# Kernel study: the 24 gate outputs of the first layer as one fp32 product in four column groups

## The chip, the cores and the metric

The kernel runs on one core of one Trainium2 chip. The metric is the device time of one execution in microseconds (us), lower is better; the median of 3 runs stands for the kernel. A separate, profiled execution gives the trace.

## The reference, cut to what matters

One inference step of a two-layer decoder trunk for 544 tokens (512 of a prompt, 8 x 4 of samples), width 1024, all in fp32. Layer 0 mixes with mLSTM heads and GLA heads, layer 1 with a Mamba-2 mixer; an MLP and layer norms follow each. Only the input projection of layer 0 matters here:

```python
mq, mk, mv, mo, mi, mf, gq, gk, gv, gg, ga = split((x @ w_in), AB_SPLITS)   # w_in: 1024 x 3096
ig = mi + ig_bias                                   # 4 columns: input gates
lf = log_sigmoid(mf + fg_bias)                      # 4 columns: forget gates
la = log_sigmoid(ga @ wa2 + ba) / GLA_TAU           # ga: 16 columns, the GLA decay
```

Of the 3096 outputs, 3072 make 24 tiles of 128 rows; the other 24 (`mi`, `mf`, `ga`) are the gates.

## The kernel before, in words

Everything is kept transposed: 128 features on the partitions, tokens along the free dimension. The 544 tokens are worked in two halves of 272 (`hf` 0 and 1). A dense product of fp32 accuracy is made of three products of a rounded type: weights and input are cut into a high and a low part (`whi`, `wlo`, `xh`, `xl`), and hi·hi, hi·lo and lo·hi are added up in PSUM. One weight tile (128 outputs, 1024 inputs, so eight blocks of K) therefore costs 24 products per half and 48 in all (`dense`, L357). The high part is made by ScalarE (a cast, L166 for weights, L286 for x), the low part by VectorE (a subtraction, L167 and L287).

`WeightStream` (L116) loads the weight tiles in a planned order through SyncE's queue into three raw buffers (`wraw`) and five pairs of cut buffers. `take_x` (L290) loads the first half of x in four pieces through ScalarE's queue, and cuts the first weight tile and these pieces by turns, a quarter of the weight tile and a quarter of x at a time. Loads on the hardware queues carry one of eight completion counters, given out by turns: a load that takes a counter up again waits until the load that had it before has landed.

The stage `ab` (L706) is the input projection with the mixer heads beside it. Its tiles go, by `order` (L821), gate, gq 0-1, gk 0-1, gv 0-3, mq, mk, mv, gg, mo. The first five tiles (`HEAD`) are worked half by half: all five for hf 0, then all five for hf 1; the others tile by tile. The gate tile is a whole weight tile of which 24 columns are used, at 0-3 (mi), 32-35 (mf) and 64-79 (ga); ScalarE evacuates it with a bias into `gate` (L797).

TensorE's instructions are in the order in which the program writes them. The mixer work is written as "lanes": generators that `tick` (L338) moves on, one step per dense product, each lane waiting as many products as its `yield` says. `warm` (L1367) is a lane too: it puts products of ones (L1372, fp32, 128x128, two records each) ahead of the first dense products and between their groups of six, so that TensorE isn't idle while data arrive. The GLA lane (L1336) waits until the gate tile is ready for both halves, waits 12 products more, and issues the decay products `la` (L1001, gate times wa2, K = 128) for q = 0 and, 12 products on, q = 1 (`gla_decay`); then it waits for the tiles gq 1 and gk 1 and goes into `gla_scores`: products `gd` (L1037), and then, every 15 dense products, one level of products `gs` (L1065).

Between `la` and the first `gs` lies a chain over three engines: ScalarE takes Abs, Exp and Ln of `la` (tile `lat`, L1002 to L1005), VectorE the minimum, a subtraction and a scan along the tokens (tile `A`, L1003 to L1007), GpSimd the difference tile `F` (L1048), ScalarE two Exp of it (L1050, L1051), and VectorE two multiplications (`zq`, L1055, and `zk`, L1057), which the first `gs` reads. ScalarE, VectorE and GpSimd have fixed orders of their own, found by the scheduler when the program is built; what they do there beside the chain are weight cuts, evacuations, masks of q (`qm`, L1032) and copies of the gate rows (`rw`, `uw`, L1184, L1185).

Of the kernel before, what the change touches and what calls it, by code (L numbers as in the profile page):

```python
# [34 lines left out]
W = dict(dec=12, gates=30, gr=8, sc=16, lev=14, v=24, kd=10, out=38, ss=40, end=12, c0=20, u=13, s=16, ml=12, mr=40, dt=238, sg=72, sx=14, sq=26, so=48, l0=12, l1=12, v0=74, v1=55, f0=16, f1=18, f2=4, ls=20, vs=47)  # L35
LEVELS = (64, 32, 16, 8, 4, 2, 1)
# [191 lines left out]
def trunk_kernel(ctx, tc, a, stages=("ab", "mlp0", "ssd", "mlp1")):  # L228
# [22 lines left out]
    for st in stages:  # L251
        if st == "ab":
            for w in [a["ab_gate"]] + [a["ab_in"][b] for b in range(24)]:
                ws.plan("ab", w)
# [35 lines left out]
    def take_x(pool, bufs=12):  # L290
# [8 lines left out]
        with tc.high_priority(), tc.manual_schedule(engines=order):  # L299
            ts = [load(S, 0, k)[0] for k in range(0, KT, 2)]  # L300
            S.preload_act_table_set("natural_log_exp_and_others")
            ws._emit([lambda k=k: cut(0, 2 * k, ts[k]) for k in range(KT // 2)])
            ws.ahead(HEAD)
            for k in range(0, KT, 2):
                t, loaded = load(nc.sync, 1, k)
                cut(1, k, t)
        with tc.issue_after(loaded):
            nc.sync.dma_start(out=lnp, in_=a["lnp"])
        return loaded
# [47 lines left out]
    def dense(w, rhs, kt, hf, evac, k0=0, ps=None):  # L357
# [6 lines left out]
        for k in range(k0, k0 + kt):  # L364
            rh, rl = rhs(k, hf)
            for wt, rt in ((hi, rh), (hi, rl), (lo, rh)):
                tick()
                last[0] = TE.matmul(ps[:, :TH], wt[:, k, :], rt, start=i == 0, stop=i == n - 1).ins  # L368
                i += 1
# [336 lines left out]
    def ab(pool, early, then):  # L706

        x_in = take_x(pool)
# [55 lines left out]
        gate = ft("gate")  # L764
        fm = {}
# [26 lines left out]
        def evac(m, hf, ps):  # L792
# [3 lines left out]
            if kind == "gate":  # L796
                S.activation(gate[:, c0:c1], ps, AF.Identity, bias=gbias)  # L797
                if hf == 1:
                    ready.add(key)
                return  # L800
# [17 lines left out]
            if hf == 1:  # L818
                ready.add(key)

        order = [("gate", 0)] + [(k, i) for k, n in (("gq", 2), ("gk", 2), ("gv", 4), ("mq", 2), ("mk", 2),  # L821
                                                     ("mv", 4), ("gg", 4), ("mo", 4)) for i in range(n)]

# [169 lines left out]
        def gla_decay():  # L993
            gla["A"] = []
            for q in range(2):
                A = ft("A")
                t = ft("lat")
                for hf in range(2):
                    c0, c1 = HALVES[hf]
                    p = pm("la")  # L1000
                    TE.matmul(p[:, :TH], wa2[:, q * P:(q + 1) * P], gate[:, c0:c1], start=True, stop=True)  # L1001
# [365 lines left out]
        def warm():  # L1367

            w = pm("warm")
            for n, gap in ((9, 6), (2, 5), (2, 5), (2, 5), (4, None)):  # L1370
                for _ in range(n):
                    TE.matmul(w[:, :P], ones, ones, start=True, stop=True)  # L1372
                if gap:
                    yield gap
# [705 lines left out]
```

## Time and profile before

| | before |
|---|---|
| median of 3 runs | 1487.77 us (1486.85 to 1490.73) |
| span of the profiled execution, first to last instruction | 1490.0 us |
| the profiled execution's time around its span | not recorded apart from the span |
| TensorE busy | 1470.5 us, 11637 products |
| VectorE / ScalarE / GpSimd busy | 1097.9 / 793.1 / 186.1 us |
| dense products of this projection, 128x128 on 272 tokens | 1200, of which 48 make the gate tile |

How to read it: PE is TensorE's products, PEld its weight loads (they overlap the products), DVE VectorE, ACT ScalarE, POOL GpSimd, SPq the queue of SyncE. Products are pipelined, so a record of 0.29 us does not mean that one takes this long: the distance between starts counts. An fp32 product that isn't cut is two records of the profile. The column in square brackets is the idle time of an engine ahead of an instruction and what ended it. `128*32` after a product's names is the part of the array it uses, rows by columns.

### The profile page before, as it was taken

To read this page: it belongs to the slowest core of one execution; us is meant where nothing else is said; L and a number is where in the kernel's file an instruction comes from. 1 tells how busy PE (TensorE), PEld (TensorE's weight loads), DVE (VectorE), ACT (ScalarE), POOL (GpSimd) and SP (SyncE) were. 2 spreads that over 40 slices of the span, in tenths; PEclk is the share of its full clock that TensorE was granted. 3 is DMA by queue.
4 is the path that set the end of the run, shared out by engine and by line. 5 is a ranking of instruction groups with operands and counts; after the bars stand their busy time and mean duration, and the time that the engine had idled before them with its cause. 6 is when DMAs were issued, how large, how long until landed. Compare 5 with 4: busy or idle time off the path is not lost.

```text
span 1490.0 us, 29251 instructions
## 1 busy us (share of the span) xinstructions
PE 1470.5 (99%) x11637; PEld 1423.8 (96%) x11637; DVE 1097.9 (74%) x2073; ACT 793.1 (53%) x1746; POOL 186.1 (12%) x224
## 2 busy tenths in 40 slices
PE   9999999999999999999999999999999999999997
PEld 9999999999999999999888789899999999999996
DVE  4956576886776766678999988777588677676656
ACT  6645556573543453547875676555257355444343
POOL 1511231100000000010233341420010000000000
PEclk9999999999999999999999999999999999999999
DMA  6321425223322322535567866364222333233221
GB/s 229 93 71 58 117 62 169 71 71 96 100 93 92 97 88 71 156 107 158 129 191 221 256 175 211 99 215 141 72 75 71 96 100 99 86 100 98 59 86 60
DMA packets 94593, 172.90 MB, mean 116 GB/s; under 512 B 15848, under 2 KB 50280, under 8 KB 94200
## 3 DMA queue, kind: packets, MB, share of 16 engines
q1 hardware_dynamic: 61848, 140.85, 30.5%
q10 hardware_dynamic: 29216, 17.19, 4.5%
q0 software_dynamic: 3392, 12.99, 2.3%
q8 instruction: 91, 1.49, 0.4%
q14 instruction: 46, 0.38, 0.1%
HBM read 153.88 MB, written 17.13 MB: 115 GB/s over the span
## 4 chain that ended last, share of the span: by engine, by line
PE 40%; DVE 5%; DMA 3%; ACT 2%; issue 1%; POOL 0%; ACTq 0%; SPq 0%; DVEq 0%; POOLq 0%
PE psd L368 27%; PE psd L580 9%; DMA E<-d_cs 1%; DVE wlo L167 1%; DVE acc L1554 1%; PE it L1707 1%; PE yp L1660 1%; ACT E L1620 1%; DVE h0n L1720 1%; DMA h0n<-h0n 1%; DMA ci<-conv 1%; PE sp L1638 1%; PE sps L1714 0%; DMA wraw<-mlp_w 0%; PE ip L1635 0%
## 5 line engine op out<-in xcount | busy, mean ns | idle before, releaser
L368 PE MATMUL psd<-xh,whi 128*128 128x272 f32 x1504 | 446.0, 297 | 0.2 <-ACT xh L286 0.2
L368 PE MATMUL psd<-xh,wlo 128*128 128x272 f32 x1504 | 440.1, 293 | 0.0
L368 PE MATMUL psd<-xl,whi 128*128 128x272 f32 x1504 | 438.3, 291 | 1.5 <-DVE xl L468 1.3
L368 PEld LDWEIGHTS psd<-xl,whi 128*128 128x128 f32 x1504 | 284.6, 189 | 7.5 <-issue 4.2
L368 PEld LDWEIGHTS psd<-xh,whi 128*128 128x128 f32 x1504 | 284.0, 189 | 7.2 <-issue 5.1
L368 PEld LDWEIGHTS psd<-xh,wlo 128*128 128x128 f32 x1504 | 283.9, 189 | 4.0 <-issue 2.8
L368 PE MATMUL psd<-hh,whi 128*128 128x272 f32 x992 | 286.5, 289 | 0.0
L368 PE MATMUL psd<-hh,wlo 128*128 128x272 f32 x992 | 286.2, 288 | 0.0
L368 PE MATMUL psd<-hlo,whi 128*128 128x272 f32 x992 | 286.1, 288 | 0.0
L167 DVE TENSOR_TENSOR wlo<-wraw,whi 128x1024 fp32r<-128x1024 f32 (+2 forms) x173 | 209.4, 1212 | 60.7 <-ACT whi L166 60.0
L166 ACT CAST whi<-wraw 128x1024 fp32r<-128x1024 f32 (+2 forms) x173 | 174.2, 1011 | 132.5 <-PE psd L368 116.6
L368 PEld LDWEIGHTS psd<-hlo,whi 128*128 128x128 f32 x992 | 186.8, 188 | 0.2
L368 PEld LDWEIGHTS psd<-hh,whi 128*128 128x128 f32 x992 | 186.8, 188 | 0.2
L368 PEld LDWEIGHTS psd<-hh,wlo 128*128 128x128 f32 x992 | 186.7, 188 | 0.1
L418 DVE TENSOR_TENSOR xf<-xf,psd 128x272 f32<-128x272 f32 x208 | 88.3, 434 | 74.8 <-PE psd L368 74.3
L580 PE MATMUL psd<-xh,wlo 128*128 128x272 f32 x416 | 119.9, 288 | 0.0
L580 PE MATMUL psd<-xh,whi 128*128 128x272 f32 x416 | 119.8, 288 | 0.0
L580 PE MATMUL psd<-xl,whi 128*128 128x272 f32 x416 | 119.6, 288 | 0.0
L202 ACT CAST whi<-wsum 128x1024 fp32r<-128x1024 f32 x52 | 54.3, 1044 | 111.3 <-PE psd L580 70.1
L202 ACT CAST whi<-wraw 128x1024 fp32r<-128x1024 f32 (+1 forms) x52 | 43.4, 834 | 95.3 <-PE psd L368 84.2
L203 DVE TENSOR_TENSOR wlo<-wsum,whi 128x1024 fp32r<-128x1024 f32 x52 | 63.7, 1224 | 23.2 <-ACT whi L202 23.2
L580 PEld LDWEIGHTS psd<-xl,whi 128*128 128x128 f32 x416 | 78.4, 188 | 0.0
(481 smaller groups left out, 2822.0 us busy)
## 6 DMA issues: line engine op xcount, KB each, us to landing
wraw<-mlp_w SPq DMA_DIRECT2D x80, 512.0 KB, 3.6
wraw<-ssd_in SPq DMA_DIRECT2D x40, 512.0 KB, 3.9
wraw<-mlp_w SPq DMA_DIRECT2D x64, 256.0 KB, 3.0
wraw<-ab_in SPq DMA_DIRECT2D x24, 512.0 KB, 3.7
h<-h SPq DMA_DIRECT2D x32, 256.0 KB, 5.2
h0n<-h0n SPq DMA_DIRECT2D x16, 512.0 KB, 6.1
E<-d_cs ACTq DMA_DIRECT2D x16, 512.0 KB, 4.7
s_h<-h0n POOLq DMA_DIRECT2D x16, 512.0 KB, 3.8
```

The lines of the kernel that those rows point to most:

```text
L166: nc.scalar.copy(hi[:, r], w[:, r])
L167: nc.vector.tensor_tensor(lo[:, r], w[:, r], hi[:, r].bitcast(F32), ALU.subtract)
L202: self.cut[0] = nc.scalar.copy(hi, x).ins
L203: self.cut[1] = nc.vector.tensor_tensor(lo, x, hi.bitcast(F32), ALU.subtract).ins
L368: last[0] = TE.matmul(ps[:, :TH], wt[:, k, :], rt, start=i == 0, stop=i == n - 1).ins
L418: V.tensor_tensor(x, x, ps, ALU.add)
L580: last[0] = TE.matmul(ps, wt[:, k], bt[:, k], start=first and n == 0, stop=n == 11, skip_group_check=not first).ins
L1554: V.scalar_tensor_tensor(acc[:, :n], ci[:, w:w + n], cw[:, m, w:w + 1], acc[:, :n], ALU.mult, ALU.add)
L1620: S.activation(E[:, r], E[:, r], AF.Exp, bias=ncs[:n, b, 8 * g + r:8 * g + r + 1])
L1638: TE.matmul(sp, Bt[:, b], xw, start=True, stop=True)
L1660: TE.matmul(ypv[64 * e:64 * e + 64, j], z[:, 64 * r:64 * r + 64], E[:, r], start=True, stop=True)
L1707: TE.matmul(it[64 + NS * k:64 + NS * k + NS], Cm[:, NS * (q + k):NS * (q + k) + NS], h0[k], start=q == 0, stop=q == NB - 2)
```

## The change

The gate tile leaves the weight stream. Its 24 columns are packed into 32 (128 KB in place of 512 KB) and loaded as `gw` in one transfer, issued on SyncE's queue between the second and third quarter of the first weight tile. The first tile is now gq 0, and the five head tiles are gq 0, gq 1, gk 0, gk 1, gv 0.

`gate_sums(hf)` makes the gates with whole fp32 products from the raw x pieces: for K block k a product of 32 output rows, written to partitions 32·(k mod 4), so that four products use four column groups of the array and each group adds up two K blocks. ScalarE copies the four partial sums to `gsum`. `gate_rows(hf)` adds the four groups and puts the rows where they belong by three small fp32 products with a matrix of stacked identities (`seye`), 4, 4 and 16 outputs at partitions 0, 32 and 64, and three evacuations with bias. For hf 0 the sums are a continuation of the lane `warm`: four products after the first six dense products and four after twelve more; the later products of ones go, and the first group of ones has ten in place of nine. For hf 1 all eight stand ahead of its first dense product. `gate_rows(0)` and `gate_rows(1)` stand ahead of the second and third head tile of hf 1.

The second weight tile is cut in four pieces (four loads, four casts, four subtractions). In the very first tile the products of two K blocks are ordered hi·hi, lo·hi for both blocks and then hi·lo for both. The `la` products read only partitions 64 to 95, K = 32.

```diff
+GATES = ((0, 0, 4), (32, 4, 4), (64, 8, 16))
...
-            for w in [a["ab_gate"]] + [a["ab_in"][b] for b in range(24)]:
-                ws.plan("ab", w)
+            for b in range(24):
+                ws.plan("ab", a["ab_in"][b])
...
-            ws._emit([lambda k=k: cut(0, 2 * k, ts[k]) for k in range(KT // 2)])
+
+            def step(k):
+                cut(0, 2 * k, ts[k])
+                if k == 1 and first is not None:
+                    first()
+            ws._emit([lambda k=k: step(k) for k in range(KT // 2)])
+            ws._emit([lambda: None] * 4)
             ws.ahead(HEAD)
...
-        for k in range(k0, k0 + kt):
+        terms = [(k, t) for k in range(k0, k0 + kt) for t in range(3)]
+        if first:
+            terms = [(k + e, t) for k in range(k0, k0 + kt, 2) for e, t in ((0, 0), (0, 2), (1, 0), (1, 2), (0, 1), (1, 1))]
+        for k, t in terms:
...
-        x_in = take_x(pool)
+        gw = pool.tile([P, KT, 32], F32, tag="sc", name="gw8", bufs=4)
+        x_in, xs_in = take_x(pool, first=lambda: nc.sync.dma_start(out=gw, in_=a["ab_gate"]))
...
+        G.memset(gate[64:96], 0.0)
...
-            if kind == "gate":
-                S.activation(gate[:, c0:c1], ps, AF.Identity, bias=gbias)
-                if hf == 1:
-                    ready.add(key)
-                return
...
+        gsum = [ft("gsum", TH) for _ in range(2)]
+
+        def gate_sums(hf):
+
+            ps = pm("gsum")
+            for k in range(KT):
+                g = k % 4
+                TE.matmul(ps[32 * g:32 * g + 32, :TH], gw[:, k], xs_in[4 * hf + k // 2][:, k % 2], start=k < 4, stop=k >= 4)
+                if k == 3 and hf == 0:
+                    yield 11
+            with tc.high_priority():
+                S.copy(gsum[hf], ps[:, :TH])
+
+        def gate_rows(hf):
+
+            c0, c1 = HALVES[hf]
+            p = pm("gates")
+            for o, c, n in GATES:
+                TE.matmul(p[o:o + n, :TH], C("seye")[:, c:c + n], gsum[hf], start=True, stop=True)
+            for o, c, n in GATES:
+                S.activation(gate[o:o + n, c0:c1], p[o:o + n, :TH], AF.Identity, bias=gbias[o:o + n])
+            if hf == 1:
+                ready.add(("gate", 0))
...
-                    TE.matmul(p[:, :TH], wa2[:, q * P:(q + 1) * P], gate[:, c0:c1], start=True, stop=True)
+                    TE.matmul(p[:, :TH], wa2[64:96, q * P:(q + 1) * P], gate[64:96, c0:c1], start=True, stop=True)
...
-            for n, gap in ((9, 6), (2, 5), (2, 5), (2, 5), (4, None)):
-                for _ in range(n):
-                    TE.matmul(w[:, :P], ones, ones, start=True, stop=True)
-                if gap:
-                    yield gap
+            for _ in range(10):
+                TE.matmul(w[:, :P], ones, ones, start=True, stop=True)
+            yield 6
+            yield from gate_sums(0)
...
         for hf in range(2):
+            for _ in gate_sums(1) if hf else ():
+                pass
             for m, w in enumerate(heads):
-                dense(w, xrhs, KT, hf, lambda h, p, m=m: evac(m, h, p))
+                if hf and 1 <= m <= 2:
+                    gate_rows(m - 1)
+                dense(w, xrhs, KT, hf, lambda h, p, m=m: evac(m, h, p), first=(hf, m) == (0, 0))
```

At the start, TensorE's instructions were in this order (`warm` products of ones, `psd` dense products of the first tile):

```order
L1372 MATMUL warm<-ones 128x128 x9
L368 MATMUL psd<-xh_72,whi 128x272
L368 MATMUL psd<-xl_74,whi 128x272
L368 MATMUL psd<-xh_72,wlo 128x272
L368 MATMUL psd<-xh_72,whi 128x272
L368 MATMUL psd<-xl_74,whi 128x272
L368 MATMUL psd<-xh_72,wlo 128x272
L1372 MATMUL warm<-ones 128x128 x2
```

and are now (`gsum` the gate sums):

```order
L1402 MATMUL warm<-ones 128x128 x10
L378 MATMUL psd<-xh_72,whi 128x272
L378 MATMUL psd<-xh_72,wlo 128x272
L378 MATMUL psd<-xh_72,whi 128x272
L378 MATMUL psd<-xh_72,wlo 128x272
L378 MATMUL psd<-xl_74,whi 128x272 x2
L838 MATMUL gsum<-xin,gw_89 32x272 x4
```

The first products that need the low part of x moved behind those that need the low part of the weights, and sums took the place of ones.

Where the GLA lane begins, in the second half of the head tiles, ScalarE's order was

```order
L166 CAST whi<-wraw 128x1024
L797 ACTIVATE gate<-psd,prm 128x272
L1184 COPY rw<-gate 4x544
L1185 COPY uw<-gate 4x544
L1002 ACTIVATE lat<-la,prm 128x272 x2
L1004 ACTIVATE lat<-lat 128x544
L166 CAST whi<-wraw 128x1024
L806 ACTIVATE gq<-psd 128x272
L1005 ACTIVATE lat<-lat 128x544
L1002 ACTIVATE lat<-la,prm 128x272 x2
L1032 ACTIVATE qm<-gq,con 128x512 x2
```

and is now

```order
L851 ACTIVATE gate<-gates,prm 16x272
L1063 ACTIVATE qm<-gq,con 128x512 x2
L1216 COPY uw<-gate 4x544
L1215 COPY rw<-gate 4x544
L1033 ACTIVATE lat<-la,prm 128x272 x2
L167 CAST whi<-wraw 128x1024
L824 COPY gk<-psd 128x272
L1033 ACTIVATE lat<-la,prm 128x272
L1035 ACTIVATE lat<-lat 128x544
L1033 ACTIVATE lat<-la,prm 128x272
L1036 ACTIVATE lat<-lat 128x544
L1035 ACTIVATE lat<-lat 128x544
```

The masks `qm` of q went ahead of the chain's first step, and both tiles' `lat` steps are interleaved behind it.

VectorE's order from the subtraction of q = 0 (`lat<-A,lat`) to the first `zk` was

```order
L1006 TENSOR_TENSOR lat<-A,lat 128x544
L1003 TENSOR_SCALAR A<-la,prm 128x272 x2
L1007 SCALAR_TENSOR_TENSOR A<-con,lat 128x544
L1101 TENSOR_SCALAR alast<-A 128x1
L167 TENSOR_TENSOR wlo<-wraw,whi 128x1024
L1006 TENSOR_TENSOR lat<-A,lat 128x544
L1055 TENSOR_TENSOR zq<-F,qm 128x512
L1007 SCALAR_TENSOR_TENSOR A<-con,lat 128x544
L167 TENSOR_TENSOR wlo<-wraw,whi 128x1024
L1057 TENSOR_TENSOR zk_532<-gk,F 128x256
```

and is now

```order
L1037 TENSOR_TENSOR lat<-A,lat 128x544
L1038 SCALAR_TENSOR_TENSOR A<-con,lat 128x544
L168 TENSOR_TENSOR wlo<-wraw,whi 128x1024
L1132 TENSOR_SCALAR alast<-A 128x1
L1037 TENSOR_TENSOR lat<-A,lat 128x544
L1070 TENSOR_TENSOR sT<-gd,con 128x4x128
L1086 TENSOR_TENSOR zq<-F,qm 128x512
L1070 TENSOR_TENSOR sT<-gd,con 128x4x128
L1088 TENSOR_TENSOR zk_540<-gk,F 128x256
```

Ahead of the first `zk` the second scan and one weight cut went out, and two evacuations of `gd` (`sT`) came in.

More of the change, by code (lines that the diff above doesn't have):

```diff
@@ L288, in split, with take_x @@
         return i.ins
-    def take_x(pool, bufs=12):
+    def take_x(pool, bufs=12, first=None):
         def load(eng, h, k):
@@ L305, in take_x @@
                 t, loaded = load(nc.sync, 1, k)
+                ts.append(t)
                 cut(1, k, t)
@@ L308, in take_x @@
             nc.sync.dma_start(out=lnp, in_=a["lnp"])
-        return loaded
+        return loaded, ts
     def new_xf(pool):
@@ L355, in flush, with dense @@
                     advance(q)
-    def dense(w, rhs, kt, hf, evac, k0=0, ps=None):
+    def dense(w, rhs, kt, hf, evac, k0=0, ps=None, first=False):
         if ps is None:
@@ L363, in dense @@
         hi, lo = w
-        for k in range(k0, k0 + kt):
+        terms = [(k, t) for k in range(k0, k0 + kt) for t in range(3)]
+        if first:
+            terms = [(k + e, t) for k in range(k0, k0 + kt, 2) for e, t in ((0, 0), (0, 2), (1, 0), (1, 2), (0, 1), (1, 1))]
+        for k, t in terms:
             rh, rl = rhs(k, hf)
[L366 to L369, printed above, removed]
+            tick()
+            last[0] = TE.matmul(ps[:, :TH], (hi, hi, lo)[t][:, k, :], (rh, rl, rh)[t], start=i == 0, stop=i == n - 1).ins
+            i += 1
         if evac is not None:
@@ L819, in evac @@
                 ready.add(key)
-        order = [("gate", 0)] + [(k, i) for k, n in (("gq", 2), ("gk", 2), ("gv", 4), ("mq", 2), ("mk", 2),
+        order = [(k, i) for k, n in (("gq", 2), ("gk", 2), ("gv", 4), ("mq", 2), ("mk", 2),
                                                      ("mv", 4), ("gg", 4), ("mo", 4)) for i in range(n)]
+        gsum = [ft("gsum", TH) for _ in range(2)]
[17 more added lines that the diff above has]
+                ready.add(("gate", 0))
         def head_out(mx, key, h, sT, enm=None):
@@ L1994, in seg @@
         return w[:, sp[n][0]:sp[n][1]]
-    g = np.zeros((D, P), w.dtype)
-    g[:, 0:4], g[:, 32:36], g[:, 64:80] = seg("mi"), seg("mf"), seg("ga")
-    o["ab_gate"] = _blocks(g, P)[0]
+    g = np.zeros((D, 32), w.dtype)
+    g[:, 0:4], g[:, 4:8], g[:, 8:24] = seg("mi"), seg("mf"), seg("ga")
+    o["ab_gate"] = _blocks(g, 32)[0]
     o["ab_in"] = _blocks(np.concatenate([seg(n) for n in ("gq", "gk", "gv", "mq", "mk", "mv", "gg", "mo")], 1), P)
```

## Prediction

> **What bounds the kernel now.** I read the engines' busy time by stretch first (columns: PE, PEld, DVE, ACT, POOL, granted clock, DMA share, GB/s):
>
> ```profile
> 14.00:30.00 16.00, 16.00 (x130) 16.00 (x129) 5.51 (x7) 7.54 (x14) 0.00 (x0) 1.00 0.74 277
> 30.00:60.00 30.00, 30.00 (x242) 29.68 (x241) 27.66 (x32) 20.90 (x45) 13.09 (x10) 1.00 0.35 107
> ```
>
> From 14 us on TensorE (PE) never stops in this projection, so a product taken out shortens the kernel by its distance to the next, unless something makes PE wait. Two things could. The start depends on data arriving. And from 30 to 60 us VectorE (DVE) is busy 27.66 of 30 us: the GLA lane's chain runs there, nearly without slack.
>
> The timeline of PE at the start (start, duration in us):
>
> ```profile
> 1.14 4.21 PE L1372 MATMUL warm<-ones 128*128 128x128 f32 x18 [1.14 <-DVE ones L280]
> 5.56 0.60 PE L368 MATMUL psd<-xh,whi 128*128 128x272 f32 x1 [0.21 <-ACT xh L286]
> 6.32 0.60 PE L368 MATMUL psd<-xl,whi 128*128 128x272 f32 x1 [0.16 <-DVE xl L287]
> ...
> 9.15 0.43 PE L368 MATMUL psd<-xh,whi 128*128 128x272 f32 x1
> 9.38 0.43 PE L368 MATMUL psd<-xl,whi 128*128 128x272 f32 x1
> ...
> 11.09 0.29 PE L368 MATMUL psd<-xh,whi 128*128 128x272 f32 x1
> 11.21 0.28 PE L368 MATMUL psd<-xl,whi 128*128 128x272 f32 x1
> ...
> 13.47 0.37 PE L368 MATMUL psd<-xh,whi 128*128 128x272 f32 x1
> ```
>
> Starts of dense products are 0.23 us apart at 9.15 and 0.12 (0.125 over longer stretches) at 11.09: PE runs at half rate until some 10.5 us, although the granted clock reads 1.00. The step came about 4 us after the last wait (0.16 us, at 6.32); the 4.21 us of products of ones before had brought none. The second tile starts at 13.47.
>
> **What goes.** From the start of the second tile on, before has 49 half tiles to do and after has 47 (the first tile's first half, gq 0 in place of the gate, is behind it in both, and the gate's second half and one half of gq 0 are saved): 48 products x 0.125 = **-6.0 us**.
>
> **What PE gets behind that point.** The prices are in two groups of rows, an fp32 product on the whole array (`la`) and sixteen in column groups (`snum`):
>
> ```profile
> 30.09 0.29 PE L368 MATMUL psd<-xh,whi 128*128 128x272 f32 x1
> 30.22 1.08 PE L1001 MATMUL la<-gate,wa 128*128 128x272 f32 x4
> ...
> 31.39 0.28 PE L368 MATMUL psd<-xh,whi 128*128 128x272 f32 x1
> ```
>
> ```profile
> 158.31 0.29 PE L368 MATMUL psd<-xh,whi 128*128 128x272 f32 x1
> 158.44 0.38 PE L934 MATMUL snum<-vstk,pbd 128*128 128x128 f32 x2
> 158.75 1.08 PE L938 MATMUL snum<-c,Zq 128*32 128x128 f32 x32
> ...
> 159.99 0.29 PE L368 MATMUL psd<-xh,wlo 128*128 128x272 f32 x1
> ```
>
> `la`: 30.09 to 31.39 is 1.30 us for three dense distances (0.375) and two fp32 products, so one of 272 tokens costs 0.46. `snum`: from 158.31 to 159.99 is 1.68; less two dense distances (0.25) and one whole fp32 product of 128 tokens (0.46 x 128/272 = 0.22) leaves 1.21 for sixteen products in four groups. One after the other they would be 16 x 0.22 = 3.5; four at a time are 0.87. So the groups do run side by side, and going into and out of them costs 1.21 - 0.87 = 0.34.
>
> By these, the sums of hf 1 (two rounds of four) cost 2 x 0.46 + 0.3 = 1.2; each `gate_rows` (three products in three groups, one round) 0.46 + 0.3 = 0.75, twice 1.5. The four `la` products keep their 0.46 each but now use a row group of 32; behind another kind of row-group products (`sc`, 4 rows) the way back to dense products shows in these rows:
>
> ```profile
> 144.47 0.39 PE L368 MATMUL psd<-xh,whi 128*128 128x272 f32 x1
> 144.70 0.28 PE L368 MATMUL psd<-xl,whi 128*128 128x272 f32 x1
> ```
>
> 144.47 to 144.70 is 0.23 in place of 0.125: 0.1 for the way out, as much taken for the way in, 0.4 for two bursts. Together **+3.1 us** (2.5 to 3.6). [...]
>
> **The start.** A new wait could come from the loads. SyncE's queue now carries two quarters, the gate weights, two quarters; with x's four pieces these are nine loads on eight counters, so the fourth quarter of the first tile, formerly issued with the others, waits for the first x piece to land.
>
> ```profile
> xin<-xT ACTq DMA_DIRECT2D x4, 272.0 KB, 5.4
> 8.87 0.72 DVE L287 TENSOR_TENSOR xl<-xin,xh 128x544 fp32r<-128x544 f32 x1
> 10.21 1.05 ACT L166 CAST whi<-wraw 128x1024 fp32r<-128x1024 f32 x1 [1.47 <-DMA wraw<-ab_in]
> ```
>
> A piece of x takes 5.4 us from issue to landing and the last cut of x ends at 8.87 + 0.72 = 9.6 before. With the quarters late, I put this cut at 9.9; until then ScalarE (ACT) and DVE alternate as they did. Then the second tile's quarters can be cut one by one (about 0.4 us each on DVE), ready from 10.4 to 11.7, where before its cast could begin only at 10.21 and took 1.05 for the whole. PE: at half rate, ten products of ones to 5.5, six dense products to 6.9, four sums 1.0, twelve dense to 10.6; then at full rate sums and six products to 12.05. That is 1.4 us ahead of 13.47. But both waits in the rows above (0.21 and 0.16) are closed, the one by the tenth product of ones, the other by the new order in the first tile. If a stretch of 4 us without a wait is what brings the full rate, it now comes by 8 us, and then the cuts bound the start and the second tile begins at about 10.5: 3.0 ahead. I take this as the likelier (3 to 2): **-3.0 us**; the other is -1.4.
>
> [...]
>
> **The wait that takes its place.** The room that the GLA chain has shrinks. Formerly the gates were ready after the first of the five second-half tiles; now they are ready after the second, while the tiles that the lane waits for next (gq 1, gk 1) are one half tile earlier. From the first `la` to `gd` there were 100 dense products; now there are 52, and 15 from there to the first `gs` as before. The chain's rows before:
>
> ```profile
> 30.13 0.64 ACT L1184 COPY rw<-gate 4x544 f32<-4x544 f32 x1
> 34.02 0.65 ACT L1005 ACTIVATE lat<-lat 128x544 f32<-128x544 f32 x1
> 35.31 1.34 ACT L1032 ACTIVATE qm<-gq,con 128x512 f32<-128x512 f32 x2
> 36.45 1.28 DVE L1007 TENSOR_TENSOR_SCAN A<-con,lat 128x544 f32<-128x544 f32 x1
> 33.86 1.23 DVE L167 TENSOR_TENSOR wlo<-wraw,whi 128x1024 fp32r<-128x1024 f32 x1 [1.08 <-ACT whi L166]
> 37.82 6.02 POOL L1048 TENSOR_TENSOR F<-A 128x512 f32<-128x512 f32 x4 [32.85 <-DVE A L1007]
> 38.16 1.78 DVE L167 TENSOR_TENSOR wlo<-wraw,whi 128x1024 fp32r<-128x1024 f32 x1 [0.23 <-ACT whi L166]
> 41.34 1.52 DVE L1055 TENSOR_TENSOR zq<-F,qm 128x512 f32<-128x512 f32 x1
> 46.03 0.42 DVE L1057 TENSOR_TENSOR zk<-gk,F 128x256 f32<-128x256 f32 x1
> 52.39 0.73 DVE L1055 TENSOR_TENSOR zq<-F,qm 128x512 f32<-128x512 f32 x1
> 48.25 1.05 PE L1065 MATMUL gs<-zq,zk 128*128 128x128 f32 x8
> ```
>
> Before, `gs` came 48.25 - 30.22 = 18.0 us after `la`, its last operand 46.45 - 30.22 = 16.2 after: slack 1.8. Now the room is 18.0 - 48 x 0.125 = 12.0, plus 0.2 of switching. The chain, from `la`: ACT first has the last gate evacuation, the masks `qm` of q = 1 (1.34) and two copies (0.64 each) to do, so `lat` starts about 2.8 us after `la`; then come the weight cast (1.05) and six steps of 0.4 to 0.65 up to the first Ln (about 4.4 in all), and the subtraction and the scan on DVE (0.7 and 1.3): the scan ends 9.2 us after `la` (before: 37.73 - 30.22 = 7.5). From there DVE has a weight cut, a subtraction, `sT`, `zq`, `sT`, `zk`, 1.23 + 4 x 0.73 + 0.42 = 4.6 us at undisturbed rates; but beside POOL's four `F` a weight cut took 1.78 for 1.23 and `zq` 1.52 for 0.73. I take the factor 1.5 over the whole: 6.9. Chain: 9.2 + 6.9 = 16.1 us in a room of 12.2: **PE waits 3.9 us at the first `gs`**, with the dense products of the following tiles behind it in its queue. Two levels on, a weight cut that slid behind the first `gs` is late by another 0.6: **+4.5 us**, between 1.0 (no slowing beside POOL: 13.8, less what ACT may gain) and 6.5 (casts that wait for PE to free a weight buffer push `lat` further).
>
> The other edits cost nothing that I can see: one more memset on POOL, which is idle for 32.85 us ahead of its first `F`; 384 KB less to load; six gate evacuations in place of two, counted in ACT's part of the chain.
>
> **The sum.** -6.0 + 3.1 - 3.0 + 4.5 = -1.4 us on the profiled execution's span of 1490.0, which is 2.2 above the median of the runs; I carry the difference over to the median: 1487.77 - 1.4 = **1486.4 us**, a chance of 0.59. About 0.3% (4.5 us) is what a measurement of this kernel can tell from no change, so this counts as no change.
>
> **Rivals.**
>
> A. *The chain keeps up* (0.24). If ACT's and DVE's items beside the chain fit into gaps, PE waits less than 1.5 us. For it: ACT's 20.90 of 30 us leave it a third. Against it: DVE's 27.66 of 30 us. Time: -5.9 with the early step and -4.3 with the late one: 1481.9 to 1483.5.
>
> B. *The wait grows and costs the full rate* (0.13). Ends on the other side. If PE waits at the first `gs` for its high end, 6.5 us, idleness as long as the stretch that brought the full rate may take it back: some 4 us at half rate, about 18 products x 0.1 = 1.8 us. Sum: -5.9 + 6.5 + 1.8 = +2.4, 1490.2; it decides from a wait of about 5.5 us on, with the late step from 4. [...]
>
>
> C. *The columns don't run side by side* (0.04): the change doesn't do what it says. Eight sums of hf 1 one after the other are 8 x 0.46 = 3.7 in place of 0.92, two `gate_rows` 1.8 more, the sums of hf 0 about 2.8 more: +7.4, 1493.8. `snum` speaks against it.
>
> **How the numbers follow.** Low end: A with the early step, 1481.9. High end: B, 1490.2; that leaves out C and what none of these cases holds. Faster by over 0.3% (under 1483.3) needs A with the early step or near it (0.24 x 2/3 = 0.16) or a wait at its low end with the early step, 0.06: 0.22. Slower by over 0.3% (over 1492.2) needs C or a B with more than one such wait: 0.07. The rest, 0.71, is no change.
>
> **What would show it.** Right: in the timeline, the second tile at 10.3 to 12.2 us; a distance of 1.1 to 1.3 us over the eight sums of hf 1; in PE's waits, the first `gs` waiting on VectorE's `zk` for 1 to 6.5 us near 40 us, which no row of PE's waits has now. Wrong: no wait of PE from 30 to 60 us (then A), PE's distances of 0.23 behind that wait (B), or sums 0.46 apart (C); also a wait at the start for gate weights or for the late quarter of the first tile, which would undo the start's gain.

## The result, and the profile after

| | before | after |
|---|---|---|
| median, first chip (5 runs each) | 1488.23 us | 1494.11 us (1493.58 to 1494.75) |
| ratio, 95% interval | | 1.0033 (1.0021 to 1.0045) |
| median, second chip (14 and 5 runs) | 1489.78 us | 1495.26 us |
| ratio, 95% interval | | 1.0045 (1.0031 to 1.0060) |
| span of the profiled execution | 1490.0 us | 1493.0 us |

The change makes the kernel slower, by 5.5 to 5.9 us between the medians (4.9 and 6.7 by the ratios). Forecast were 1.4 us less, within 1481.9 to 1490.2. A span leaves out some 1.7 us that a time holds (1493.0 and 1494.75 for one execution), so spans go with spans. The two profiled executions differ by 3.0 us only, and that gap between 3.0 and 5.9 turned out to be a finding of its own.

The start first. The timeline of TensorE, after (start, duration):

```profile
6.25 0.43 PE L378 MATMUL psd<-xh,wlo 128*128 128x272 f32 x1
6.48 0.66 PE L378 MATMUL psd<-xl,whi 128*128 128x272 f32 x2
7.06 0.78 PE L838 MATMUL gsum<-xin,gw 128*32 128x272 f32 x8
...
8.00 0.28 PE L378 MATMUL psd<-xh,wlo 128*128 128x272 f32 x1
8.12 0.29 PE L378 MATMUL psd<-xh,whi 128*128 128x272 f32 x1
...
9.26 0.29 PE L378 MATMUL psd<-xh,wlo 128*128 128x272 f32 x1
9.54 0.52 PE L378 MATMUL psd<-xl,whi 128*128 128x272 f32 x2
...
11.44 0.29 PE L378 MATMUL psd<-xh,whi 128*128 128x272 f32 x1
```

Products are 0.23 us apart at 6.25 and 0.125 at 8.00, so the full rate came at about 7 us; forecast was by 8 us. The second tile starts at 11.44, not at 10.5. ScalarE and VectorE show why:

```profile
7.77 0.41 ACT L167 CAST whi<-wraw 128x256 fp32r<-128x256 f32 x1 [1.41 <-DMA wraw<-ab_in]
8.76 0.73 DVE L288 TENSOR_TENSOR xl<-xin,xh 128x544 fp32r<-128x544 f32 x1
9.74 0.72 DVE L288 TENSOR_TENSOR xl<-xin,xh 128x544 fp32r<-128x544 f32 x1
```

The third quarter of the first weight tile now stands behind the gate weights on SyncE's queue and lands late: its cast waits 1.41 us and begins at 7.77, where before had it at 6.58. The third piece of x is cut behind it, the products that read its `xl` begin at 9.54, and the sums and the last six products follow. The last cut of x ends at 10.46; forecast was 9.9. This is a wait of the kind that the prediction's last sign of being wrong names.

The new work between 23 and 60 us, and the waits in it:

```profile
23.56 1.12 PE L838 MATMUL gsum<-xin,gw 128*32 128x272 f32 x16
27.81 0.65 PE L849 MATMUL gates<-gsum,con 128*4 128x272 f32 x6
31.59 0.65 PE L849 MATMUL gates<-gsum,con 128*4 128x272 f32 x6
33.99 1.38 PE L1032 MATMUL la<-gate,wa 32*128 32x272 f32 x4
37.12 1.18 PE L1032 MATMUL la<-gate,wa 32*128 32x272 f32 x4
...
48.50 1.16 PE L1096 MATMUL gs<-zq,zk 128*128 128x128 f32 x8 [1.47 <-DVE zk L1088]
52.38 1.16 PE L1096 MATMUL gs<-zq,zk 128*128 128x128 f32 x8 [0.84 <-DVE zk L1088]
```

The sums do run side by side (16 records in 1.12 us). The chain's wait is there, at the place that was named, but 2.3 us in place of 4.5. On VectorE the end of the chain, and the second scan ahead of the next `gs`:

```profile
41.94 1.29 DVE L1038 TENSOR_TENSOR_SCAN A<-con,lat 128x544 f32<-128x544 f32 x1
...
46.34 0.93 DVE L1086 TENSOR_TENSOR zq<-F,qm 128x512 f32<-128x512 f32 x1
...
47.79 0.66 DVE L1088 TENSOR_TENSOR zk<-gk,F 128x256 f32<-128x256 f32 x1
48.37 2.18 DVE L1038 TENSOR_TENSOR_SCAN A<-con,lat 128x544 f32<-128x544 f32 x1
```

PE's waits from 30 to 240 us (us in all, times, longest), where before has no row at all:

```profile
PE gs L1096 <- DVE zk L1088: 2.3, 2, 1.5
PE hot L899 <- ACT hn L893: 1.7, 3, 0.7
PE md L1314 <- ACT kz L1310: 0.8, 1, 0.8
```

The last two rows are in no step of the prediction: transposes (`hot`) and the score products (`md`) of the heads wait for ScalarE near 125 and 195 us. The third thing that was not forecast shows in the windows (PE, PEld, DVE, ACT, POOL, granted clock, DMA share, GB/s):

```profile
30.00:60.00 30.00, 27.69 (x210) 25.17 (x209) 22.83 (x29) 21.46 (x45) 12.83 (x10) 1.00 0.31 88
...
110.00:240.00 130.00, 127.41 (x1026) 119.30 (x1025) 83.72 (x293) 70.44 (x179) 27.34 (x38) 0.97 0.27 82
```

```profile
146.00:148.00 2.00, 2.00 (x15) 1.83 (x14) 0.55 (x4) 0.00 (x0) 0.00 (x0) 0.82 0.03 8
148.00:150.00 2.00, 2.00 (x11) 2.00 (x11) 0.32 (x3) 0.23 (x1) 0.00 (x0) 0.50 0.00 0
150.00:152.00 2.00, 2.00 (x15) 2.00 (x15) 0.72 (x1) 1.33 (x2) 0.40 (x1) 0.83 0.00 0
198.00:200.00 2.00, 2.00 (x10) 1.66 (x10) 1.45 (x3) 0.45 (x2) 0.49 (x1) 0.62 0.00 0
200.00:202.00 2.00, 2.00 (x8) 1.56 (x7) 0.79 (x3) 0.00 (x0) 1.17 (x3) 0.53 0.00 0
```

The granted clock is 0.97 from 110 to 240 us, because it falls to 0.50 twice, for 3.4 us each time (147.3 to 150.7, and 198.5 to 201.9). I call that a half-rate stretch. (In every profile TensorE also falls idle and to half rate in the last 5 to 8 us; that is left out below.) One costs 15 products x 0.1 = 1.5 us if it is filled with dense products.

### The profile page after: what moved, and what is told of

Same layout as the page of the kernel before. It is cut to its first block, busy times and chain, and to the rows that moved or that the text cites. A ratio compares the mean times of both kernels' runs of the same rounds, so it can differ in the third digit from the quotient of the medians.

```text
span 1493.0 us, 29232 instructions
## 1 busy us (share of the span) xinstructions
PE 1468.9 (98%) x11615; PEld 1417.0 (95%) x11615; DVE 1096.6 (73%) x2075; ACT 795.1 (53%) x1754; POOL 191.5 (13%) x225
## 4 chain that ended last, share of the span: by engine, by line
PE 42%; DVE 4%; DMA 2%; issue 1%; ACT 1%; POOL 0%; SPq 0%; DVEq 0%; POOLq 0%; ACTq 0%
PE psd L378 29%; PE psd L590 9%; DVE wlo L168 1%; PE yp L1694 1%; DMA ec<-d_ecs 1%; DVE acc L1588 1%; PE it L1741 1%; DMA E<-d_cs 1%; PE sp L1672 1%; DMA wraw<-mlp_w 0%; PE sps L1748 0%; DVE h0n L1754 0%; PE ip L1669 0%; ACT E L1654 0%; PE xt L1633 0%
## 5 line engine op out<-in xcount | busy, mean ns | idle before, releaser
L378 PEld LDWEIGHTS psd<-xh,whi 128*128 128x128 f32 x1488 | 280.9, 189 | 9.2 <-issue 6.9
L378 PEld LDWEIGHTS psd<-xh,wlo 128*128 128x128 f32 x1488 | 280.8, 189 | 4.2 <-issue 3.2
```

What stands on the lines that cost most here:

```text
L378: last[0] = TE.matmul(ps[:, :TH], (hi, hi, lo)[t][:, k, :], (rh, rl, rh)[t], start=i == 0, stop=i == n - 1).ins
```

## The experiments

The theory that I went in with: what was forecast as gain is there, and is given back in three places, the wait at `gs` (2.3 us), the waits of `hot` and `md` (2.5 us), and half-rate stretches. Rivals: each wait may have a cause other than the one I name, the stretches may be bound to the new products rather than to chance, and the start's edits may do harm. Each ratio is against the kernel before on the same chip, whose median was 1489.3 to 1489.8 us there. "End of the first stage" below is the start of the last transposed state product (`mkt`): 230.39 in before's first profile, 234.83 in after's.

**Do the gates come too late? (e1)** The change ahead of the second half of gq 0, both halves of the gates at once:

```diff
-                if hf and 1 <= m <= 2:
-                    gate_rows(m - 1)
+                if hf and m == 1:
+                    gate_rows(0)
+                    gate_rows(1)
```

> The changed kernel, with both gate_rows ahead of the second half of gq 0, so that the gates and la come 24 dense products (3.0 us) earlier and the GLA chain has 76 products of room in place of 52. My theory (the gain on paper is there, but is given back in three places: the GLA chain at the first gs, 2.3 us; the sample lane against the ml heads, 2.5 us; half-rate stretches of TensorE, 3.4 us): PE's wait at the first gs goes or falls under 0.5 us, the waits of hot and md stay, and the time falls by 2 us to about 1492.0; as all that lies behind gs comes some 2 us earlier, the half-rate stretches may lie elsewhere, which is worth 1.7 us each either way. Rival (the wait is set by the chain's later part, scan and zk beside the weight cuts, and not by when the gates come): the wait stays above 1.5 us and the time within 1 us of the changed kernel, 1494.

Measured: 1498.39 us, 1.0057 (1.0045 to 1.0069). The first `la` came 3.3 us earlier (30.73) and the wait grew:

```profile
47.25 0.28 PE L378 MATMUL psd<-xl,whi 128*128 128x272 f32 x1
51.11 2.07 PE L1096 MATMUL gs<-zq,zk 128*128 128x128 f32 x8 [3.57 <-DVE zk L1088]
52.84 0.57 PE L378 MATMUL psd<-xh,wlo 128*128 128x272 f32 x1
53.21 0.43 PE L378 MATMUL psd<-xh,whi 128*128 128x272 f32 x1
53.43 0.43 PE L378 MATMUL psd<-xl,whi 128*128 128x272 f32 x1
```

My theory fell, in the rival's direction: with `la` earlier, the scheduler put a weight cut and the second scan on VectorE in front of `zq` and `zk`. The rows show a second thing: behind 3.57 us of waiting the distances are 0.23. This is the prediction's rival B, at another length of wait than the 5.5 us that it named: the clock falls at 49.5, 2.0 us into the wait. Two half-rate stretches follow each other here (49.5 to 56.3), and e1 has two more, at 199.7 and 844.8, and a new wait of 0.7 us at `la`, for the gates' evacuation.

**Are `hot` and `md` a matter of place? (e2, e3)** The tile series and the mLSTM heads stand 48 dense products earlier than before, since a tile is gone; the GLA lane with its heads and samples stands only 24 earlier. Products issued ahead of each:

| | before | after | four head tiles (e2) | samples late (e3) |
|---|---|---|---|---|
| first `hot` of the GLA heads | 605 | 581 | 557 | 605 |
| GLA samples, first `snum` | 817 | 793 | 769 | 842 |
| mLSTM heads, first `md` | 907 | 859 | 859 | 907 |

In e2, the first stage works four head tiles half by half in place of five; gq and gk come sooner by that, and the GLA lane stands 48 products earlier too (the text on record says four in place of three; the edit is four in place of five):

```diff
-        heads = [ws.next() for _ in range(HEAD)]
+        heads = [ws.next() for _ in range(HEADA)]    # HEADA = 4
```

> The changed kernel, with four tiles at the head of the projection in place of three (gk 1 too), which brings every lane's place 24 products earlier and so sets the GLA samples against the ml heads as the kernel before has them. My theory: the waits of hot and md (2.5 us) go, with them the second half-rate stretch near 198 us (1.7 us); the wait at the first gs stays at about 2.3 or falls, since gk 1 now lies ahead of la. Time 1490 (1489.5 to 1492). Rival (the waits of hot and md come from the lanes being nearer to the end of the first stage, not from their place against each other): the waits stay at 2 us or more and the time within 1 us of 1494.

Measured: 1491.55 us, 1.0015 (1.0006 to 1.0023). PE's waits from 30 to 240 us are now one row:

```profile
PE gs L1097 <- DVE zk L1089: 2.3, 2, 1.5
```

`hot` and `md` wait no more, and of the stretches only one is left (143.6 to 147.0). e3 is the kernel before with one line, `yield 24` ahead of the GLA samples:

> The kernel before, with the GLA samples 24 products later and nothing else: the phase of the sample lane against the ml heads is shifted by as much as the change shifted it the other way. My theory, that each collision of the two lanes is a matter of phase, leaves open whether this way collides; if it does, PE gets waits at hot, md or the sample products of 1 to 3 us, and a half-rate stretch of 1.7 us may follow; time 1488 to 1493. Rival (the phase is without weight, and the waits of the changed kernel come from its longer ScalarE and VectorE work): no new wait over 0.3 us, time within 1 us of the kernel before, 1488.2.

Measured: 1493.49 us, 1.0028 (1.0018 to 1.0038). PE's waits from 30 to 240 us:

```profile
PE hot L868 <- ACT hn L862: 2.0, 1, 2.0
PE md L1283 <- ACT kz L1279: 0.5, 1, 0.5
```

The kernel before, with nothing of the change in it, gets waits at the same two places near 195 us from a shift of 24 products, and no half-rate stretch in this profile. Taken away in e2 and made in e3, the cause of these waits is shown: the samples' place against the heads. (The 0.7 us at `hot` near 125 goes in e2 too, but e3 doesn't make it.) ScalarE's order tells how, in after:

```profile
194.75 1.15 ACT L893 ACTIVATE hn<-num,hb,hf 128x128 f32<-128x128 f32 x3
195.78 0.44 ACT L817 ACTIVATE gg<-gg 128x272 f32<-128x272 f32 x1
196.10 0.47 ACT L893 ACTIVATE hn<-num,hb,hf 128x128 f32<-128x128 f32 x1
```

and in before:

```profile
192.94 1.51 ACT L862 ACTIVATE hn<-num,hb,hf 128x128 f32<-128x128 f32 x4
```

The heads' work and a tile's evacuation (`gg`) meet on ScalarE, which is not busy on the average (70.44 of 130 us), only at that place.

**Do the stretches move? (e4, e8)** e4 puts four fp32 products of ones behind the sums of hf 1; e8 has 36 in place of 8 dense products between the two groups of thin products (`sc`, 4 rows of the array) that stand ahead of the stretch at 147.

```diff
+            if hf:                                     # e4
+                w1 = pm("warm")
+                for _ in range(4):
+                    TE.matmul(w1[:, :P], ones, ones, start=True, stop=True)
...
-            yield W["gr"]                              # e8, between the two groups of sc
+            yield 36
```

> The changed kernel, with four fp32 products of ones (about 0.21 us each) behind the sums of the second half of the gate tile, so that all of PE's later work up to the first wait comes 0.86 us later. [...] Rival (the half rate follows directly from the work, wherever it lies on the clock): the same two stretches stand 0.9 us later and the time is 1495.0.

> The changed kernel, with 36 in place of 8 dense products between the two groups of the sample rows' products (sc, of four rows), so that they can't fall into one stretch of 3.4 us. [...]

Measured: e4 1494.41 us, 1.0036 (1.0023 to 1.0048); e8 1495.53 us, 1.0034 (1.0022 to 1.0046). In both, the stretch at 147 is gone and the one near 198 stays; e4's `hot` waits 2.7 in place of 1.7 us, and e8 has a new stretch at 842. No gain in either, and for e8, which I had put at about 1492.5, that is a miss. Neither settles what brings a stretch: the changed kernel itself lost the one at 147 when it ran again (e10, e16 below). The records of the granted clock tell where they stand. In after, the clock is 0.50 from 147.28 to 150.69 and from 198.48 to 201.89, 3.41 us each time. The second one begins at 196.05 in e16 and at 196.81 in e8, and those two have one more each, at 841.17 and 841.93: near the same work, but not at the same time. The sixteen records of `sc` begin between 144.00 us and the fall at 147.28 in after's first profile, though TensorE isn't idle there, and between 139.92 and the fall at 143.58 in e2; in e7 half rate follows them too (144.85). In the other fifteen profiles none follows them. That is a pattern over these executions; what makes it isn't shown.

**What is the start worth? (e5, e12)** The kernel before with the change's start alone, without the gate weights' load and the sums: the second tile in quarters, the first tile's order, ten products of ones, no last group.

```diff
+            ws._emit([lambda: None] * 4)
...
-            for n, gap in ((9, 6), (2, 5), (2, 5), (2, 5), (4, None)):
+            for n, gap in ((10, 6), (2, 5), (2, 5), (2, None)):
```

> The kernel before, its gate tile kept, with only the change's start: the second tile's weights cut in quarters, the first tile's new order of products, ten products of ones ahead and no last group of four. My theory (the start is worth what the data allow, the second tile beginning near 11.4 us whatever the clock does): second tile at 11.3 to 12.0 us, time 1.5 to 2.1 us under the kernel before, no new wait behind it, and no more than one half-rate stretch more or less (1.7 us). Rival (the start's edits are what brings the half-rate stretches, by moving the full rate's step): new half-rate stretches in the first stage and a time at or over the kernel before.

> The kernel with the new start alone, once more, for a second profile. Its first had a first stage 2.9 us shorter and no shorter time. If the ssd stage takes such a gain back (VectorE bounds its first third), the distance from the first head's transposes there (721.1) to the first state product (766.4) is again 45 us or more where the kernel before has 43 to 44. If that was chance, it is 44 or less and the span 1485 to 1486.

Measured: e5 1489.50 us, 1.0002 (0.9994 to 1.0011); e12, one execution, 1488.66, within the range of before's runs on that chip (1488.58 to 1492.28). The second tile began at 10.26 and 10.21, a microsecond ahead of what was on record (11.3 to 12.0) and of the changed kernel: without the gate weights ahead of it the third quarter's cast begins at 6.39 and 6.57, and the last cut of x ends at 9.43 and 9.39. The first stage ended at 227.5 and 227.7, 2.9 and 2.7 us ahead of before's first profile, and the time didn't move. Both theories for e5 were wrong on that: nothing new waits in the first stage, no stretch lies there (e5 has one at 836), and e12 has none.

**Which start is before's usual one? (e10, e11, e13 to e16)** Unedited kernels, profiled again.

> The changed kernel once more, beside the kernel before on one chip. If the account of the first profile holds (2.3 us at gs, 2.5 us at hot and md, which are in the program and come every time, and half-rate stretches, which are drawn anew in each execution), the three waits stand as they were to 0.2 us, the half-rate stretches may lie elsewhere, and the time is 1493 to 1495, 1.0025 to 1.004 of the kernel before. If the waits themselves are chance, they differ by over 0.5 us.

> The kernel before once more, for a second profile of it. If its first profile, which had a half-rate stretch behind the wait of 2.2 us at 724 us and a span 2.2 us over the median, was unlucky there, the second has no stretch at that place, the first stage to within 0.3 us as it was (first transposed state product at 228.6 us), and a span of 1486 to 1488. If the stretch belongs to the kernel, it stands there again.

> The kernel before, a third profile, for the start alone. The two profiles so far differ by 1.9 us at the end of the first stage and by nothing else in it: the full rate came at 10.5 us in the first and earlier in the second. [...] Rival (the start of the first profile is the usual one): 13.3 to 13.6 us in at least two of the three.

> The kernel before, a fourth profile; expectations as for the third.

> The kernel before, a fifth profile; expectations as for the third.

> The changed kernel, a third profile. My theory: its second tile starts at 11.3 to 11.7 us wherever the step falls, since the last cut of x sets it; the waits at gs, hot and md are 2.3, 1.7 and 0.8 us again, and only the half-rate stretches move. Rival (the start of the changed kernel depends on the step as well): the second tile moves by more than 0.5 us.

| | second tile starts | first stage ends | span | half-rate stretches |
|---|---|---|---|---|
| before, first profile | 13.47 | 230.4 | 1490.0 | 724 |
| before, e11 | 11.65 | 228.5 | 1490.3 | 761 |
| before, e13 | 11.21 | 228.2 | 1487.3 | 722 |
| before, e14 | 11.38 | 228.3 | 1486.4 | 722 |
| before, e15 | 11.29 | 228.2 | 1486.8 | 722 |
| after, first profile | 11.44 | 234.8 | 1493.0 | 147, 198 |
| after, e10 | 11.34 | 231.6 | 1490.7 | 727 |
| after, e16 | 11.46 | 233.2 | 1493.6 | 196, 841 |

The timeline of e13 at the start, against the rows of before in the prediction:

```profile
6.07 0.39 PE L368 MATMUL psd<-xl,whi 128*128 128x272 f32 x1 [0.37 <-DVE xl L287]
6.30 0.29 PE L368 MATMUL psd<-xh,wlo 128*128 128x272 f32 x1
6.42 0.29 PE L368 MATMUL psd<-xh,whi 128*128 128x272 f32 x1
...
10.40 1.06 PE L1372 MATMUL warm<-ones 128*128 128x128 f32 x8
11.21 0.37 PE L368 MATMUL psd<-xh,whi 128*128 128x272 f32 x1
```

The waits at `gs`, `hot` and `md` are 2.3, 1.7 and 0.8 us in all three profiles of after, to 0.1: they belong to the program. The stretches move: of what was put on record for e11, neither the first stage to 0.3 us nor a stretch at the old place came true. e10's time, 1495.26 us, came out just over what was on record for it (1493 to 1495).

With a longer wait (0.37) at 6.07 than the first profile had, e13 runs at full rate from the first dense product on. The first profile, with its step at 10.5 us, was the odd one of five. (e3, whose start is that of before, has the late step too: 10.7 us, second tile at 13.35.) Four of five starts lie at 11.2 to 11.65 us, where the changed kernel's start lies too; those of e13 to e15 are just under the 11.4 to 13.6 us that I had expected of them. The step falls elsewhere from execution to execution: ahead of 5.3 us in e13, near 7 in e11, at 10.5 in the first. Half rate came later too. PE's longest wait in before's first profile is (us in all, times, longest)

```profile
PE xt L1599 <- DVE ncs L1515: 2.2, 1, 2.2
```

and behind the same wait, at 722 us, e13 has

```profile
721.94 1.09 PE L1599 MATMUL xt<-scon,Y 128*128 128x128 f32 x4 [2.23 <-DVE ncs L1515]
722.82 0.64 PE L1601 MATMUL cb<-Cf,Bf 128*128 128x128 f32 x2
...
723.48 0.43 PE L368 MATMUL psd<-xh,wlo 128*128 128x272 f32 x1
723.71 0.43 PE L368 MATMUL psd<-xh,whi 128*128 128x272 f32 x1
...
725.20 0.29 PE L368 MATMUL psd<-xl,whi 128*128 128x272 f32 x1
```

a half-rate stretch. By the clock it begins at 721.66, when the wait had lasted 1.95 us. All eighteen profiles have this wait of 2.2 us. In five of them half rate follows, 1.95 us or more after the wait began; in the thirteen others none follows. What decides isn't shown.

The stretch costs next to nothing there: from `xt` to the first state product `it` the five profiles with it (four of before, e10) take 44.2 to 44.5 us, the twelve without a stretch in this part 44.0 to 45.2. VectorE is busy 41.4 of 44 us there (e13) and PE waits for it; that it sets the pace is likely, not shown. The part also takes back what a shorter first stage gains: in e5, e12 and e9 (below), whose first stages end 0.6 to 1.4 us ahead of before's usual 228.3, `it` starts at 766.2 to 766.4, and in e13 to e15 at 766.1 to 766.2.

**Can the change be made to pay? (e6, e7, e9)** On the kernel of e2: e6 puts `la` on the whole array again; e7, on e6, emits the decay of q = 1 behind the second level of q = 0; e9, on e7, holds ScalarE's gate copies and the masks of q = 1 behind the first Ln.

```diff
-        G.memset(gate[64:96], 0.0)                                                       # e6
+        G.memset(gate, 0.0)
-  TE.matmul(p[:, :TH], wa2[64:96, q * P:(q + 1) * P], gate[64:96, c0:c1], ...)
+  TE.matmul(p[:, :TH], wa2[:, q * P:(q + 1) * P], gate[:, c0:c1], ...)
...
+                    if n == 3:                                                           # e7, in gla_scores
+                        next(dec)
...
-            S.copy(z, gate[32:36])                                                       # e9, in ml_gates
-            S.copy(u, gate[0:4])
+            with hold("lat"):
+                S.copy(z, gate[32:36])
+                S.copy(u, gate[0:4])
```

> The kernel with four head tiles, with the la products on the whole array again (the gate tile zeroed, 128 rows with the weights' zero rows) in place of a row group of 32. My theory (the row group costs 1.0 us over the two bursts, 2.6 us of extra distance in place of 1.8, and not the 0.4 of the prediction): the two bursts take 0.9 us each again and the time falls by about 0.8 to 1.0 us against the kernel with four head tiles (1491.55), half-rate stretches apart. Rival (the bursts wait for the gate's evacuation and only seem longer): the bursts stay as long, no gain.

> As the one before, with la and the decay of q = 1 emitted behind the second level of q = 0 in place of ahead of the first gs, so that VectorE has neither the second scan (2.2 us) nor its two preparations (2.4 us) between the first scan and zk. My theory (the wait at gs is VectorE's queue between scan and zk, not the time at which the gates come): PE's wait at gs falls from 2.3 to under 0.5 us and the time by 1.8 to 2.3 us against the kernel with la on the whole array. Rival (the chain is bound ahead of the scan, by ScalarE): the wait stays over 1.5 us.

> The kernel with the decay of q = 1 behind the second level, and in addition ScalarE's two gate copies and the masks of q = 1 held behind the first Ln, so that neither ScalarE nor VectorE has foreign work between the first la and zk but weight casts. My theory (the chain from la to the first gs is as long as what the two queues hold in front of its steps, about 14.6 us so far whenever la comes): the chain shortens to about 12 us, PE's wait at gs falls from 3.1 to under 0.7 us, the samples' state products stand 2 us or more earlier than in the kernel with la on the whole array, and the first stage ends 4 us before that of the kernel before. At the end of the kernel the time is 1486 to 1488 if the first stage's gain lasts. Rival (a gain of the first stage is taken back in the ssd stage, as the kernel with the new start alone suggests): the first stage is 4 us shorter and the time still 1488 to 1490.

Measured: e6 1490.77 us, 1.0009 (1.0000 to 1.0017): the bursts give back 0.6 us of the forecast 0.8 to 1.0; the time is 0.8 less than e2's, which the intervals don't separate. The wait at `gs` is 2.0 us there, and half rate begins 1.0 us behind it, at 47.0. e7 1492.44 us, 1.0020 (1.0011 to 1.0028), a miss: the wait at `gs` rose from 2.0 to 3.1, since ScalarE now had a second weight cast ahead of Ln and VectorE a second cut ahead of the scan, so that the scan began 2.5 us later than in e6 (41.92 for 39.45). e9 1488.27 us, 0.9992 (0.9982 to 1.0001), with VectorE's queue between scan and `zk`

```profile
36.99 1.29 DVE L1039 TENSOR_TENSOR_SCAN A<-con,lat 128x544 f32<-128x544 f32 x1
38.31 0.15 DVE L1137 TENSOR_SCALAR alast<-A 128x1 f32<-128x1 f32 x1
38.42 2.06 DVE L169 TENSOR_TENSOR wlo<-wraw,whi 128x1024 fp32r<-128x1024 f32 x1
40.41 1.52 DVE L1089 TENSOR_TENSOR zq<-F,qm 128x512 f32<-128x512 f32 x1
41.85 1.26 DVE L1091 TENSOR_TENSOR zk<-gk,F 128x256 f32<-128x256 f32 x1
```

and PE's waits at `gs` down to 0.3 and 0.3 us: from `la` (31.30) to the end of `zk` (43.1) the chain takes 11.8 us in place of 14.5. Its first stage ends at 226.9, 1.4 us ahead of before's usual 228.3, and its median is 1.5 us less. On record were 4 us at the end of the first stage, measured against before's first profile, and a time of 1486 to 1488; the time is that of the rival (1488 to 1490). It beats the changed kernel clearly and can't be told from the kernel before. The chain's place is thereby shown, and its lever too: not when `la` comes (e1) nor how much follows the scan (e7), but what stands ahead of each of its steps in two queues.

## Why the prediction was wrong

The sum can be made in one place without chance: from the start of the second tile to the end of the first stage, in e14 of before and e10 of after, which have no half-rate stretch there. That is 216.9 us before and 220.2 after, +3.3. By the prediction's terms, from the distances between PE's starts:

| term | forecast | measured |
|---|---|---|
| 48 dense products less | -6.0 | -6.0 |
| sums of hf 1 / two `gate_rows` / `la` | +1.2 / +1.5 / +0.4 | +1.26 / +1.54 / +0.97 |
| wait at `gs` | +4.5 | +2.3, and 0.65 in the distances about it |
| `hot` and `md` | none | +2.5, and 0.6 about them |
| smaller differences (the remainder) | none | -0.5 |
| start | -3.0 | 0.0 against the usual start, -2.0 against the first profile |

1. **What goes** was right to 0.1 us.
2. **What PE gets** was right for the column groups and short by 0.6 for `la`: the price of going in and out of another shape was read from a burst of four-row products (0.2 us a burst), and a row group of 32 costs 0.5. What the way in and out costs depends on the burst here, 0.2 to 0.5 us.
3. **The start** failed twice. Mis-sized: the last cut of x, put at 9.9 us, ends at 10.4 to 10.5, and the second tile starts at 11.3 to 11.5 and not at 10.5. The prediction had the fourth quarter of the first tile late (in after, SyncE's queue waits 2.0 us for x to land and issues it at 4.63); the gate weights make the third one late as well (1.4 to 1.5 us of waiting on ScalarE in three profiles), and the sums and six products still follow the products that waited for it. Without gate weights and sums the second tile starts at 10.2 (e5, e12). That a stretch of some 4 us without a wait brings the full rate, on which the choice of 10.5 rested, was an estimate from one execution, and no run shows it: e13 had the full rate with a wait of 0.37 us at 6.07. And counted against the wrong start: the gain was taken against an execution that began its second tile 1.8 to 2.3 us later than the other four of before, so that most of it was in the median already. Against the usual start the gain is nothing. (The prediction put that execution 2.2 us over the median by setting a span against a time; with the 1.7 us that a span leaves out in the other runs it was some 3.5 to 3.9 over. What the start doesn't explain of this came behind 680 us, and its cause is open.) With the waits of `hot` and `md` the start makes up most of the distance between -1.4 and the result: with 0 for -3.0, all else as forecast, the sum is +1.6.
4. **The wait that takes its place** had the right place and mechanism at half its size. From `la` to the end of the chain 16.1 us were forecast, and 14.5 measured (33.99 to 48.45, the end of `zk`). The front came as forecast (the scan ends at 43.23, 9.2 us behind `la`); the part behind the scan took 5.2 in place of 6.9, and the room was 13.0 in place of 12.2. The second wait (0.84) stands behind the scan of q = 1, not behind a weight cut. Rival A (no wait) and rival C (sums one after the other) are both out by this and by the 1.12 us of the sums. The factor 1.5 for work beside GpSimd was right for some steps and not for others (0.93 and 1.50 us for two `zq` rows of after, against 0.73 undisturbed).
5. **"The other edits cost nothing that I can see"** is the step that failed outright. The order of work was followed for the lane's front end only. That the GLA lane moves by 24 products and everything else by 48 was there to be read in the order, and it makes 2.5 us of waits at 125 and 195 us, on an engine that is about half busy (e2, e3).
6. **Rival B** had half rate behind a wait, with too high a bar (it came 1.95 us into the wait at 722 in e13, and in e6 1.0 us behind the 2.0 us at `gs`; 5.5 us were not needed), some 4 us for its length where 3.4 were measured, and no price for where it strikes. In the three profiles of the changed kernel it didn't follow the wait at `gs`; it came behind the thin `sc` products (147) and behind short waits (198): none, one or two such stretches in the first stage, at 1.5 us or a little more each, and one more at 841. Where such a stretch follows the wait at 722, as all of before's do but one, it costs next to nothing; the one at 761 (e11) goes with the longest span of the five.

Sum against the median, an estimate from three profiles: +3.3 for the first stage and about 2 for stretches that cost (four in three profiles, x 1.6 / 3) is 5.4; 5.5 and 5.9 were measured.

The chance of 0.07 for slower by over 0.3% was too small for a plain reason: only the terms that lower the time had been asked what they rest on.

## What to carry to other kernels

Before a sum is made against a profiled execution that is longer than the median, find where its excess lies; if it lies at the place that the change touches, the gain there is already in the median. When a change takes out a unit of a pipelined order, list how far each lane moves; lanes that move by different amounts meet other work than they met before, and the waits come far from the edit. A wait on a chain through in-order queues is shortened by what is put behind it in those queues, not by starting it earlier.

## What the runs showed of the hardware

- TensorE fell to half rate for 3.4 us at a time: 1.95 us into the 2.23 us wait of e13 (at 722), behind 0.59, 0.34 and 0.80 us of waiting within some 3 us (after, from 195), and 2.0 us into the 3.57 us wait of e1, the longest one but for the end of the kernel.
- The length of a wait alone doesn't tell whether a drop follows. All eighteen profiles have the wait of 2.2 us at 722 us; a drop follows it in five and not in thirteen. After's drop at 198.48 came with 1.73 us of waiting in all.
- At the start (0 to 14 us of before) the granted clock reads 1.00 while the distances are those of half rate (0.23 us); later drops show in it as 0.50 (after, 147.28 to 150.69). The start's rate is read from distances.
- In e1 one weight cut on VectorE took 1.20 us (at 41.98) and the next of the same shape 2.06 (at 44.58), both with GpSimd's `F` under way by the trace: the slowing beside GpSimd is no constant factor.
